# Differential attention: plain identity transposes, 1/sum moved into the next norm, and the product with V in plain float32

## The chip, the core and the metric

One core of a Trainium2 chip runs the whole program as one launch. The metric is the device time of one execution in microseconds. The three runs of the kernel before took 3952.47 us in the median (3940.81 to 3964.31).

## What is computed

Two blocks in a row. The first (a Hyena and a gated recurrent mixer, then 16 experts) is not touched. The second has two layers over 1024 latent tokens and 256 context tokens; four heads, each with two score maps, and a norm over the 128 values of each head behind them:

```python
def rms_norm(t, g):
    y = tf * lax.rsqrt(jnp.mean(tf * tf, axis=-1, keepdims=True) + EPS)
...
def diff_attend(q, k, v, lam):
    s = jnp.einsum('bhmqd,bhmkd->bhmqk', q, k).astype(jnp.float32) * (QK_DIM ** -0.5)
    p = jax.nn.softmax(s, axis=-1)
    p = p[:, :, 0] - lam * p[:, :, 1]
    return jnp.einsum('bhqk,bhkd->bhqd', p.astype(v.dtype), v)

def attn_post(o, subln_g, lam_init):
    o = rms_norm(o, subln_g) * (1.0 - lam_init)
```

The latent queries see 256 context keys and 1024 latent keys. In the first layer the context also attends to itself (256 queries, 256 keys).

## The kernel before

The program is written as tiles in pools with a fixed number of buffers; a scheduler lists the instructions of each engine in an order made at build time, and each engine then runs its list in order. `interleave` and generators set in which order the text hands out the work; a tile's buffer is handed on when its readers are done.

Nearly all products are made from halves: a float32 operand is split into a rounded part (F32R, by ScalarE in `split`, line 184) and the remainder (VectorE or GpSimd, line 187), and `mm3` (lines 204 to 206) adds three rounded matmuls. `mm` (line 209) is one matmul; with plain float32 operands it leaves two records in a trace, with F32R operands one. `tr` (line 212) is the transpose of a block by the identity. In names like `po<-th,Vh` the first operand moves, the second is the one held in the array.

`lat_path` runs the two latent layers. Each first projects v, q and k (`v_rows`, `qk_rows`) and makes the two side branches (`side_ct`), then come attention and the gate projection together, then the output projection with the norm (`gated_y`, `out_pair`). The context attention, `ctx_rest`, runs inside the expert layer, beside `moe`.

`lat_operands` loads K and V of one head. K is split into two stacked operands (KA), V into Vh and Vl, through `u2` tiles that hold the raw loads. All loads go over SP's queue in order (`self.dma`).

`attention` walks over blocks of 256 queries, 4 a head, 16 a layer. In each, for two groups of 128 queries and both maps: scores in pieces of 512, 512 and 256 keys (tile `s`, six matmuls), a VectorE copy with the scale and a running minimum (`E`, line 1515), the minimum over the pieces, the exponential on ScalarE with its sum (line 181), then 1/sum (line 1522) and the difference of the two maps: on VectorE for the second group, on ScalarE and GpSimd for the first. Then, for five pairs of key tiles, the weights are turned: four matmuls by a diagonal matrix `dg` that holds -1/sum, made on GpSimd from a negated identity (`nident`); so the turning also scales. The turned block `pt` is split into `th` (ScalarE) and `tl` (VectorE), and six matmuls add it times V into `po`:

```python
                        self.mm(pt[:, kk, i * 128:i * 128 + 128], Ps[i][:, (kp + kk) * 128:(kp + kk) * 128 + 128], dgs[i])
...
                self.cp(th, pt)
                self.tt(tl, pt, th.bitcast(F32), SUB)
...
                    self.mm3(po, V[0][:, kt], V[1][:, kt], th[:, kk], tl[:, kk], kt == 0, kt == nkt - 1)
```

Between these steps `next(fill, None)` hands out one step of the gate projection (`gate_steps`: three matmuls of 512 columns, tile `po<-T`); 24 of its 128 steps stand ahead of the attention (`FRONT`), 9 are called for in each block. `gated_y` takes the attention's output of 256 tokens, sums the squares per head and token, makes the root of the mean plus eps (`rstd`) and scales by it and by `sub`, which is subln_g times (1 - lam_init).

Of the kernel before, what the change touches and what calls it, by code (L numbers as in the profile page):

```python
# [9 lines left out]
F32 = mybir.dt.float32  # L10
F32R = mybir.dt.float32r
# [9 lines left out]
EPS = 1e-6  # L21
# [109 lines left out]
class Work:  # L131
# [1304 lines left out]
    def ctx_operands(self, h):  # L1436

        KA = [self.t("cKA", [128, 256], F32R) for _ in range(2)]
        QA = [self.t("cQA", [128, 256], F32R) for _ in range(2)]
        QB = [self.t("cQA", [128, 256], F32R) for _ in range(2)]  # L1440
        V = (self.t("cV", [128, 2, 128], F32R), self.t("cV", [128, 2, 128], F32R))
        k, q, v = (self.t("cu", [128, 256]) for _ in range(3))
# [4 lines left out]
        v = v.rearrange("p (a b) -> p a b", a=2)  # L1447
        self.dma(v, self.dvc[0, h])
        self.split(v, *V)
        return KA, lambda qb: (QA, QB), V, self.rqc[h]  # L1450

    def ctx_qk(self, l, q, h, hT, w="w"):
# [6 lines left out]

    def lat_operands(self, l, h):  # L1460
        KA = [self.t("KA", [128, 1280], F32R) for _ in range(2)]
        V = (self.t("Vh", [128, 10, 128], F32R), self.t("Vl", [128, 10, 128], F32R))
        kc = self.t("u2", [128, 256])
        self.dma(kc, self.dkc[l, h])
        self.put_qk(kc, KA, None, slice(0, 256))
        for t0 in range(0, 1024, 512):
            kt = self.t("u2")
            self.dma(kt, self.dqk[h, 1][:, t0:t0 + 512])
            self.put_qk(kt, KA, None, slice(256 + t0, 768 + t0))
        q = self.t("qf")  # L1470
        self.dma(q, self.dqk[h, 0])
        vc = self.t("u2", [128, 2, 128])
        self.dma(vc, self.dvc[l, h])
        self.split(vc, V[0][:, 0:2], V[1][:, 0:2], self.nc.gpsimd)
        for t0 in range(0, 8, 4):
            vt = self.t("u2", [128, 4, 128])
            self.dma(vt, self.dv[h][:, t0:t0 + 4])
            s = slice(2 + t0, 6 + t0)
            self.split(vt, V[0][:, s], V[1][:, s], self.nc.gpsimd)

        def queries(qb):
            QA = [self.t("QA", [128, 256], F32R) for _ in range(2)]
# [6 lines left out]
    def attention(self, l, n, nk, ops, dst, c, fill=()):  # L1489


        fill = iter(fill)
        nc = self.nc
        KA, queries, V, rq = ops
        nkt = nk // 128
        chunks = [(k0, min(k0 + 512, nk)) for k0 in range(0, nk, 512)]
        nc_ = len(chunks)
        for qb in range(n // 256):
            QA, QB = queries(qb)
            Ps, dgs = [], []  # L1500
            for i in range(2):
                qs = slice(i * 128, i * 128 + 128)
                es = []
                mx = self.sm([128, 2, nc_ + 1], "a3")
                ss = self.sm([128, 2], "a2")
                rc = self.sm([128, 2], "a2")
                for m in range(2):
                    r = rq[:, qb * 2 + i, m:m + 1]
                    mc = mx[:, m, nc_:nc_ + 1]
                    E = self.t(c + "E%d" % m, [128, nk])  # L1510
                    for j, (k0, k1) in enumerate(chunks):
                        o = self.ps(c + "s", [128, k1 - k0])
# [7 lines left out]
                    self.act(E, E, AF.Exp, scale=-1.0, bias=mc, accum_out=ss[:, m:m + 1])  # L1520
                    es.append(E)
                nc.vector.reciprocal(rc, ss)  # L1522
                self.stt(rc[:, 1:2], rc[:, 1:2], self.lams[l], ss[:, 0:1], MUL, MUL)
                dg = self.t(c + "dg", [128, 128])
                self.ts(dg, self.nident, rc[:, 0:1], MUL, eng=nc.gpsimd)
                if c or i:
                    self.stt(es[0], es[1], rc[:, 1:2], es[0], MUL, SUB)
                else:
                    self.act(es[1], es[1], AF.Copy, scale=rc[:, 1:2])
                    self.tt(es[0], es[1], es[0], SUB, nc.gpsimd)  # L1530
                Ps.append(es[0])
                dgs.append(dg)
# [158 lines left out]
            lo.append(l_)  # L1691
        return hi, lo

    def gated_y(self, l, t0, dy, dg, pt, tag, ytag, tmp):

        hi, lo = [], []
        tsl = slice(t0, t0 + 256)
        for cc in range(2):
# [5 lines left out]
            if cc:  # L1704
                pm = self.ps(pt, [128, 2, 4])
                for c2 in range(2):
                    sq = self.t(tmp, [128, 2, 256])
                    self.act(sq, y[:, c2 * 2:c2 * 2 + 2], AF.Square)
                    for i in range(2):
                        for hh in range(2):  # L1710
                            h = c2 * 2 + hh
                            self.mm(pm[:, i, h:h + 1], sq[:, hh, i * 128:i * 128 + 128], self.ones[:, 0:1])
                rs = self.sm([128, 2, 4], "gy")
# [67 lines left out]
            self.dma(self.f256, I["k_f256"])  # L1781

    def prep2(self, pt, tmp):
        self.nident = self.cst([128, 128], name="nident")
        self.ts(self.nident, self.ident, -1.0, MUL)
# [45 lines left out]
    def ctx_rest(self):  # L1831
# [1 line left out]
        dyc, dgc = self.dyc, self.dgc  # L1833
        P_ = self.nc.gpsimd
        with ExitStack() as e:
            self.open(e, "right", cKA=4, cQA=6, cV=4, cE0=2, cE1=2, cdg=2, cth=1, ctl=1, cot=1)
            for h in range(4):
                yield from self.attention(0, 256, 256, self.ctx_operands(h), dyc[4 + h], "c")
        with ExitStack() as e:
            self.open(e, "right", cy=4)  # L1840
            y = self.gated_y(0, 0, dyc, dgc, "cp", "cy", "Tc", "cv")
# [65 lines left out]
    def lat_path(self, hT, rope, ec, e0, e1):  # L1907
# [3 lines left out]
        for l in range(2):  # L1911
# [22 lines left out]
                        self.side_ct(l, 1024, hT, dy, SH.index(h), "sp", "su", "sw", "sz")  # L1934
            ec.close()
            Tl = "T%d" % l
            with ExitStack() as e2:
                self.open_ps(e2, "left", po=2, pt=2, s=4)
                self.open(e2, "left", KA=4, qf=2, QA=8, E0=4, E1=2, u2=3, wr=2, wh=2, wl=2, gu=2,
                          Vh=2, Vl=2, dg=4, th=2, tl=2, ot=2, gb=1)  # L1940
                gate = self.gate_steps(l, 1024, hT, dg, "po", "gu", "w", self.nc.gpsimd)
                for _ in range(FRONT):
                    next(gate)
                for h in range(4):
                    ops = self.lat_operands(l, h)
                    for _ in self.attention(l, 1024, 1280, ops, dy[4 + h], "", gate):
                        pass
                for _ in gate:
                    pass
# [4 lines left out]
            with ExitStack() as e2:  # L1954
                self.open_ps(e2, "left", pp=3, pq=5)
                self.open(e2, "left", y4=5, yt=6, xr=3, u2=4)
                dst = self.dram([1024, 1024], name="x3") if l == 0 else self.out[0]
                gy = lambda t0: self.gated_y(l, t0, dy, dg, "pq", "y4", "yt", "u2")
# [226 lines left out]
```

## Time and profile before

| | |
|---|---|
| runs (3) | 3952.47 us median, 3940.81 to 3964.31 |
| the profiled execution | 3952.19 us, its span 3950.4 us |
| TensorE busy (PE) | 3602.6 us, 91% |
| VectorE (DVE) / ScalarE (ACT) / GpSimd (POOL) busy | 2909.2 / 2305.5 / 1293.6 us |
| moved by DMA | 824.40 MB, mean 209 GB/s |
| latent attention, layer 0 | 2830 to 3165 us |
| latent attention, layer 1 | 3512 to 3844 us |

Busy time of TensorE counts overlapping matmuls once; a matmul's own duration includes its way through the array, so its price in a row of matmuls is the distance of their starts. "PEclk" is the granted TensorE clock, 1.00 for the full 2.4 GHz, 0.50 for 1.2 GHz; a value between is a mean over time. "Idle before" is time in which the engine waited, with what ended it.

### The profile page before, as it was taken

The page shows a single profiled execution, that of the slowest core. Times are in us where ns is not written, and L with a number is a line of the kernel's source. Part 1 is how long each engine was busy: PE and PEld are TensorE (multiplying, and loading weights), DVE is VectorE, ACT ScalarE, POOL GpSimd, SP SyncE. Part 2 cuts the span into 40 slices and gives each one's busy share as a digit, 9 for nine tenths or more (in the row PEclk, how much of TensorE's full clock was granted, in tenths as well). Part 3 has the DMA queues.
Part 4 walks back from the last instruction along what each step waited for, and adds up shares of the span by engine and source line. Part 5 has one row for each costly group of instructions (what it writes and reads, how often), then busy time and mean ns, then how long its engine had stood idle before and what let it go on. Part 6 is the DMA issues. An engine that isn't in the chain of part 4 may idle for free. (4 is left out here: it accounts for less than half of the span.)

```text
span 3950.4 us, 54906 instructions
## 1 busy us (share of the span) xinstructions
PE 3602.6 (91%) x18922; PEld 2940.1 (74%) x18922; DVE 2909.2 (74%) x4414; ACT 2305.5 (58%) x3757; POOL 1293.6 (33%) x940
## 2 busy tenths in 40 slices
PE   6999899768897899999999999879999899999989
PEld 2667688646866778787777777678788788878878
DVE  4587778898635898889888888855677744567772
ACT  4443433355534787778777777665566654566762
POOL 3455655454413313230121120101444620143461
PEclk7999999879998999999999999989999999999989
DMA  7777767645376699999999999951311244131033
GB/s 230 224 220 222 221 211 222 212 165 190 115 253 204 213 330 350 351 323 352 365 355 365 365 353 364 318 179 52 121 50 39 71 139 120 60 119 58 33 102 112
DMA packets 530527, 824.40 MB, mean 209 GB/s; under 512 B 38193, under 2 KB 241991, under 8 KB 530248
## 3 DMA queue, kind: packets, MB, share of 16 engines
q1 hardware_dynamic: 503176, 755.74, 56.0%
q0 software_dynamic: 26048, 64.09, 6.0%
q8 instruction: 149, 2.44, 0.3%
q10 hardware_dynamic: 1024, 1.06, 0.2%
q14 instruction: 130, 1.06, 0.1%
HBM read 712.65 MB, written 107.05 MB: 207 GB/s over the span
## 5 line engine op out<-in xcount | busy, mean ns | idle before, releaser
L187 DVE TENSOR_TENSOR el<-er,eh 128x1024 fp32r<-128x1024 f32 x763 | 953.5, 1299 | 99.0 <-ACT eh L184 97.1
L184 ACT ACTIVATE eh<-er 128x1024 fp32r<-128x1024 f32 x768 | 785.5, 1057 | 128.3 <-PE ea L206 86.0
L205 PE MATMUL ea<-el,xh 128*128 128x512 f32 x1024 | 416.2, 406 | 22.9 <-DVE el L187 20.6
L206 PE MATMUL ea<-eh,xh 128*128 128x512 f32 x1024 | 405.2, 396 | 0.0
L204 PE MATMUL ea<-eh,xh 128*128 128x512 f32 x1024 | 404.3, 398 | 0.2 <-ACT eh L184 0.2
L1284 POOL DMA_INDIRECT acc<-yo,idx x16 | 76.6, 4786 | 761.8 <-DVE yo L196 761.8
L1515 DVE TENSOR_SCALAR_CACHE_REDUCE E<-s,rq 128x512 f32<-128x512 f32 (+1 forms) x384 | 239.1, 657 | 51.4 <-PE s L209 37.1
L205 PEld LDWEIGHTS ea<-el,xh 128*128 128x128 f32 x1024 | 192.7, 188 | 91.3 <-DVE el L187 50.6
L181 ACT ACTIVATE E<-E,a 128x1280 f32<-128x1280 f32 x160 | 216.6, 1359 | 57.0 <-DVE a L1519 52.9
L209 PE MATMUL s<-KA,QA 128*128 128x512 f32 (+1 forms) x768 | 203.0, 387 | 26.7 <-DVE E L1515 26.0
L204 PEld LDWEIGHTS ea<-eh,xh 128*128 128x128 f32 x1024 | 192.7, 188 | 46.0 <-ACT eh L184 0.9
L206 PEld LDWEIGHTS ea<-eh,xh 128*128 128x128 f32 x1024 | 193.0, 188 | 38.7
L205 PE MATMUL ey<-el,hh 128*128 128x512 f32 x512 | 205.3, 401 | 3.4 <-DVE el L187 3.3
L204 PE MATMUL ey<-eh,hh 128*128 128x512 f32 x512 | 202.7, 403 | 4.2 <-ACT eh L184 4.0
L206 PE MATMUL ey<-eh,hh 128*128 128x512 f32 x512 | 202.2, 395 | 0.0
L209 PE MATMUL pt<-dg,E 128*128 128x128 f32 x1280 | 181.9, 288 | 10.6 <-DVE E L196 4.5
L184 ACT ACTIVATE u<-pp 32x512 f32<-32x512 f32 (+2 forms) x212 | 124.2, 587 | 99.3 <-PE pp L206 93.0
L204 PE MATMUL pp<-T,ah 128*128 128x512 f32 x448 | 180.4, 403 | 0.0
L209 PEld LDWEIGHTS pt<-dg,E 128*128 128x128 f32 x1280 | 168.6, 203 | 15.8 <-issue 11.9
L205 PE MATMUL pp<-T,ah 128*128 128x512 f32 x448 | 177.8, 397 | 0.0
L206 PE MATMUL pp<-T,al 128*128 128x512 f32 x448 | 177.3, 396 | 0.0
L187 POOL TENSOR_TENSOR wl<-wr,wh 128x1024 fp32r<-128x1024 f32 (+1 forms) x48 | 117.6, 2459 | 179.2 <-ACT wh L184 177.8
(535 smaller groups left out, 10003.8 us busy)
## 6 DMA issues: line engine op xcount, KB each, us to landing
er<-in_exp_w_dram SPq DMA_DIRECT2D x768, 512.0 KB
wr<-in_w_in_dram SPq DMA_DIRECT2D x60, 512.0 KB
dc<-in_k_dft_dram POOLq DMA_DIRECT2D x72, 384.0 KB, 4.4
dc<-in_k_dft_dram POOLq DMA_DIRECT2D x72, 256.0 KB, 4.4
ar<-in_w_in_dram SPq DMA_DIRECT2D x64, 256.0 KB
mr<-in_w_mod_dram SPq DMA_DIRECT2D x48, 256.0 KB
wr<-in_ada_w_dram SPq DMA_DIRECT2D x24, 512.0 KB
wr<-in_w_out_dram SPq DMA_DIRECT2D x24, 512.0 KB
```

The costliest lines, as they stand in the source:

```text
L181: return self.nc.scalar.activation(out, in_, func, **kw)
L184: return self.nc.scalar.activation(out, in_, AF.Copy)
L187: return (eng or self.nc.vector).tensor_tensor(out, a, b, op=op)
L204: mm(out, lh, rh, start=first, stop=False)
L205: mm(out, lh, rl, start=False, stop=False)
L206: mm(out, ll, rh, start=False, stop=last)
L209: self.nc.tensor.matmul(out, l, r, start=first, stop=last)
L1284: nc.gpsimd.indirect_dma_start(out=self.acc, out_offset=x[0], in_=yo, in_offset=None, compute_op=ADD)
L1515: nc.vector.tensor_scalar(E[:, k0:k1], o, r, None, op0=MUL, op1=ALU.min, accum_out=mx[:, m, j:j + 1] if nc_ > 1 else mc)
```

## The change

The transposes use the identity and carry no scale. The two maps are combined as (lambda x sum0/sum1) x E1 - E0, which is minus sum0 times the wanted weights; the sign goes into `sub` (lam_init - 1). The factor sum0 cancels in the norm behind, if its eps is multiplied by sum0 squared: so the sums are kept in a constant tile `s0` per layer, and `gated_y` uses eps x s0 x s0, by two more small VectorE operations and a square root without its bias. V is loaded once, unsplit; `th` stays plain float32; `tl`, `dg`, `Vh`, `Vl` and `nident` are gone; the product with V is one `mm` per key tile in place of `mm3`. `th` has 4 buffers instead of 2.

```diff
@@ ctx_operands and lat_operands: V
-        V = (self.t("Vh", [128, 10, 128], F32R), self.t("Vl", [128, 10, 128], F32R))
+        V = self.t("V", [128, 10, 128])
+        self.dma(V[:, 0:2], self.dvc[l, h])
+        self.dma(V[:, 2:10], self.dv[h])
...
-        vc = self.t("u2", [128, 2, 128])
-        self.dma(vc, self.dvc[l, h])
-        self.split(vc, V[0][:, 0:2], V[1][:, 0:2], self.nc.gpsimd)
-        for t0 in range(0, 8, 4):
-            vt = self.t("u2", [128, 4, 128])
-            self.dma(vt, self.dv[h][:, t0:t0 + 4])
-            s = slice(2 + t0, 6 + t0)
-            self.split(vt, V[0][:, s], V[1][:, s], self.nc.gpsimd)
@@ attention
-                ss = self.sm([128, 2], "a2")
-                rc = self.sm([128, 2], "a2")
+                sums = [s0[:, qb * 2 + i:qb * 2 + i + 1], self.sm([128, 1], "a2")]
+                rc = self.sm([128, 1], "a2")
...
-                nc.vector.reciprocal(rc, ss)
-                self.stt(rc[:, 1:2], rc[:, 1:2], self.lams[l], ss[:, 0:1], MUL, MUL)
-                dg = self.t(c + "dg", [128, 128])
-                self.ts(dg, self.nident, rc[:, 0:1], MUL, eng=nc.gpsimd)
+                nc.vector.reciprocal(rc, sums[1])
+                self.stt(rc, rc, self.lams[l], sums[0], MUL, MUL)
...
-                        self.mm(pt[:, kk, i * 128:i * 128 + 128], Ps[i][:, (kp + kk) * 128:(kp + kk) * 128 + 128], dgs[i])
-                th = self.t(c + "th", [128, 2, 256], F32R)
-                tl = self.t(c + "tl", [128, 2, 256], F32R)
+                        self.tr(pt[:, kk, i * 128:i * 128 + 128], Ps[i][:, (kp + kk) * 128:(kp + kk) * 128 + 128])
+                th = self.t(c + "th", [128, 2, 256])
                 self.cp(th, pt)
-                self.tt(tl, pt, th.bitcast(F32), SUB)
...
-                    self.mm3(po, V[0][:, kt], V[1][:, kt], th[:, kk], tl[:, kk], kt == 0, kt == nkt - 1)
+                    self.mm(po, V[:, kt], th[:, kk], kt == 0, kt == nkt - 1)
@@ gated_y
-                self.rstd(rs, pm, 128, "gy")
+                rs, sd = (self.sm([128, 2, 4], "gy") for _ in range(2))
+                i0 = t0 // 128
+                si = s0[:, :, i0:i0 + 2].rearrange("p h i -> p i h")
+                self.stt(sd, si, EPS, si, MUL, MUL)
+                self.stt(rs, pm, 1.0 / 128, sd, MUL, ADD)
+                self.act(sd, rs, AF.Sqrt)
+                self.nc.vector.reciprocal(rs, sd)
@@ prep2
-            self.ts(s, self.colb("subln_g_2", l), 1.0 - LAM_INIT[l], MUL)
+            self.ts(s, self.colb("subln_g_2", l), LAM_INIT[l] - 1.0, MUL)
@@ lat_path
-                          Vh=2, Vl=2, dg=4, th=2, tl=2, ot=2, gb=1)
+                          V=2, th=4, ot=2, gb=1)
```

The scheduler makes a new order. TensorE at the end of layer 0's attention (last block of the last head; `pt` the turned weights, `E` the weights, `po` the sum with V), first before:

```order
L209 MATMUL pt_29981<-dg_29878,E_7466_29846 128x128
L209 MATMUL pt_29981<-dg_29917,E_7478_29885 128x128
L204 MATMUL po_29920<-th_29971,Vh_29293 128x256
L205 MATMUL po_29920<-tl_29972,Vh_29293 128x256
L206 MATMUL po_29920<-th_29971,Vl_29294 128x256
L204 MATMUL po_29920<-th_29971,Vh_29293 128x256
L205 MATMUL po_29920<-tl_29972,Vh_29293 128x256
L206 MATMUL po_29920<-th_29971,Vl_29294 128x256
```

and the same place now:

```order
L212 MATMUL pt_29319<-ident_116,E_7321_29221 128x128
L212 MATMUL pt_29319<-ident_116,E_7332_29258 128x128
L209 MATMUL po_29291<-th_29315,V_28781 128x256 x2
L212 MATMUL pt_29328<-ident_116,E_7321_29221 128x128
L212 MATMUL pt_29328<-ident_116,E_7332_29258 128x128
```

Six matmuls behind two tiles, th and tl, have become two (x2) behind one, and the transposes of the next pair still stand between them.

SP's queue ahead of the attention of layer 0 (`qf` the queries, `u` from dkc and dqk the keys, `u` from dvc and dv the values, all of head 0, but the second qf of head 1), before:

```order
L177 DMA qf_26789<-dqk_24849 128x1024
L177 DMA qf_27634<-dqk_24849 128x1024
...
L177 DMA u_6700_26771<-dkc_10007 128x256
L177 DMA u_6701_26777<-dqk_24849 128x512
...
L177 DMA u_6704_26791<-dvc_10009 128x256
L177 DMA u_6705_26795<-dv_24850 128x512
```

and now:

```order
L177 DMA V_26698<-dvc_10009 128x256
L177 DMA V_26698<-dv_24787 128x1024
...
L177 DMA V_27396<-dvc_10009 128x256
L177 DMA V_27396<-dv_24787 128x1024
...
L177 DMA qf_26719<-dqk_24786 128x1024
L177 DMA qf_27417<-dqk_24786 128x1024
```

The loads of V of heads 0 and 1 have moved from behind the key loads to ahead of the query loads.

## Rows read from the trace of the kernel before

**Rows 1.** The page, first line.
```profile
span 3950.4 us, 54906 instructions
```

**Rows 2.** Busy time by stretch: us, engines (instructions), PEclk, DMA share, GB/s.
```profile
2830.00:3165.00 335.00, 302.77 (x1821) 263.26 (x1820) 250.24 (x659) 221.70 (x357) 165.27 (x110) 0.95 0.20 65
3512.00:3844.00 332.00, 301.11 (x1820) 263.21 (x1819) 253.43 (x657) 224.15 (x360) 169.80 (x112) 0.94 0.21 66
...
2830.00:2870.00 40.00, 30.64 (x124) 23.62 (x123) 28.82 (x82) 27.04 (x43) 21.86 (x17) 0.83 0.41 129
2870.00:3080.00 210.00, 201.97 (x1252) 176.88 (x1250) 158.09 (x418) 138.80 (x229) 89.69 (x64) 0.99 0.15 49
3080.00:3165.00 85.00, 70.17 (x450) 62.77 (x449) 63.33 (x161) 55.87 (x86) 53.72 (x30) 0.90 0.23 73
```

**Rows 3.** PE's waits in layer 0: us in total, times, longest.
```profile
PE s L209 <- DVE E L1515: 13.4, 10, 2.8
PE po L205 <- DVE tl L187: 8.1, 8, 4.2
PE po L204 <- ACT th L184: 4.0, 5, 1.9
```

**Rows 4.** PE's waits in layer 1.
```profile
PE po L205 <- DVE tl L187: 10.8, 8, 4.2
```

**Rows 5.** Timeline of PE, layer 0: start, length, line, out<-in, shape, count.
```profile
2899.84 0.28 PE L204 MATMUL po<-th,Vh 128*128 128x256 f32 x1
2899.96 0.28 PE L205 MATMUL po<-tl,Vh 128*128 128x256 f32 x1
...
2906.73 1.73 PE L209 MATMUL pt<-dg,E 128*128 128x128 f32 x14
2908.21 0.48 PE L205 MATMUL po<-T,wh 128*128 128x512 f32 x1
2908.52 0.39 PE L206 MATMUL po<-T,wl 128*128 128x512 f32 x1
2908.75 0.63 PE L209 MATMUL s<-KA,QA 128*128 128x512 f32 x2
```

**Rows 6.** PE's groups by shape in layer 0: records, busy us, mean ns, idle before.
```profile
L209 PE MATMUL pt<-dg,E 128*128 128x128 f32 x640 | 90.9, 287 | 5.3 <-DVE E L196 2.2 <-DVE a L1522 2.0 <-POOL E L187 0.8
L209 PE MATMUL s<-KA,QA 128*128 128x512 f32 x256 | 85.1, 431 | 9.5 <-DVE E L1515 8.9 <-DVE KA L187 0.4
L205 PE MATMUL po<-tl,Vh 128*128 128x256 f32 x160 | 48.9, 306 | 8.3 <-DVE tl L187 8.1
...
L204 PE MATMUL po<-T,wh 128*128 128x512 f32 x105 | 42.1, 401 | 0.5 <-ACT ot L184 0.5
```

**Rows 7.** Timeline of PE, transposes in the output stage of layer 0.
```profile
3203.21 1.25 PE L212 MATMUL pq<-ident,y 128*128 128x128 f32 x10
3204.22 0.48 PE L205 MATMUL pp<-T,yt 128*128 128x512 f32 x1
3204.54 0.40 PE L206 MATMUL pp<-T,yt 128*128 128x512 f32 x1
```

**Rows 8.** Timeline of PE, plain float32 with 256 columns, first stage.
```profile
134.83 10.63 PE L209 MATMUL pp<-c,cr 128*128 128x256 f32 x48
```

**Rows 9.** VectorE's group tl in layer 0.
```profile
L187 DVE TENSOR_TENSOR tl<-pt,th 128x512 fp32r<-128x512 f32 x80 | 54.6, 686 | 29.3 <-ACT th L184 29.2
```

**Rows 10.** Timeline of PE, tail of layer 0.
```profile
3099.36 0.58 PE L205 MATMUL po<-tl,Vh 128*128 128x256 f32 x1 [4.22 <-DVE tl L187]
```

**Rows 11.** ScalarE's group Vh in layer 0.
```profile
L184 ACT ACTIVATE Vh<-u 128x512 fp32r<-128x512 f32 x8 | 5.0, 620 | 7.2 <-DMA u<-dv 7.2
```

**Rows 12.** Timeline of ScalarE, a table load at layer 0's end.
```profile
3158.09 1.28 ACT L181 ACT_TABLE_LOAD   x1
```

**Rows 13.** Busy time by stretch, in the expert layer.
```profile
2350.00:2450.00 100.00, 96.92 (x427) 75.81 (x426) 90.12 (x83) 76.08 (x92) 19.08 (x5) 1.00 1.01 355
```

**Rows 14.** Timeline of PE, transposes behind a long idle time.
```profile
2582.86 3.92 PE L212 MATMUL fp<-ident,xn 128*128 128x128 f32 x16 [25.29 <-DVE xn L192]
```

More of the change, by code (lines that the diff above doesn't have):

```diff
@@ L1440, in ctx_operands @@
         QB = [self.t("cQA", [128, 256], F32R) for _ in range(2)]
-        V = (self.t("cV", [128, 2, 128], F32R), self.t("cV", [128, 2, 128], F32R))
-        k, q, v = (self.t("cu", [128, 256]) for _ in range(3))
+        V = self.t("cV", [128, 2, 128])
+        k, q = (self.t("cu", [128, 256]) for _ in range(2))
         self.dma(k, self.dkc[0, h])
@@ L1446, in ctx_operands @@
         self.put_qk(q, QA, QB, slice(0, 256))
-        v = v.rearrange("p (a b) -> p a b", a=2)
-        self.dma(v, self.dvc[0, h])
-        self.split(v, *V)
+        self.dma(V, self.dvc[0, h])
         return KA, lambda qb: (QA, QB), V, self.rqc[h]
@@ L1487, in lat_operands, with attention @@
         return KA, queries, V, self.rq[h]
-    def attention(self, l, n, nk, ops, dst, c, fill=()):
+    def attention(self, l, n, nk, ops, dst, s0, c, fill=()):
         fill = iter(fill)
@@ L1499, in attention @@
             QA, QB = queries(qb)
-            Ps, dgs = [], []
+            Ps = []
             for i in range(2):
@@ L1519, in attention @@
                         nc.vector.tensor_reduce(mc, mx[:, m, :nc_], axis=AX.X, op=ALU.min)
-                    self.act(E, E, AF.Exp, scale=-1.0, bias=mc, accum_out=ss[:, m:m + 1])
+                    self.act(E, E, AF.Exp, scale=-1.0, bias=mc, accum_out=sums[m])
                     es.append(E)
-                nc.vector.reciprocal(rc, ss)
-                self.stt(rc[:, 1:2], rc[:, 1:2], self.lams[l], ss[:, 0:1], MUL, MUL)
-                dg = self.t(c + "dg", [128, 128])
-                self.ts(dg, self.nident, rc[:, 0:1], MUL, eng=nc.gpsimd)
+                nc.vector.reciprocal(rc, sums[1])
+                self.stt(rc, rc, self.lams[l], sums[0], MUL, MUL)
                 if c or i:
-                    self.stt(es[0], es[1], rc[:, 1:2], es[0], MUL, SUB)
+                    self.stt(es[0], es[1], rc, es[0], MUL, SUB)
                 else:
-                    self.act(es[1], es[1], AF.Copy, scale=rc[:, 1:2])
+                    self.act(es[1], es[1], AF.Copy, scale=rc)
                     self.tt(es[0], es[1], es[0], SUB, nc.gpsimd)
                 Ps.append(es[0])
-                dgs.append(dg)
             po = self.ps(c + "po", [128, 256])
@@ L1692, in w_gated, with gated_y @@
         return hi, lo
-    def gated_y(self, l, t0, dy, dg, pt, tag, ytag, tmp):
+    def gated_y(self, l, t0, dy, dg, s0, pt, tag, ytag, tmp):
         hi, lo = [], []
@@ L1712, in gated_y @@
                             self.mm(pm[:, i, h:h + 1], sq[:, hh, i * 128:i * 128 + 128], self.ones[:, 0:1])
-                rs = self.sm([128, 2, 4], "gy")
-                self.rstd(rs, pm, 128, "gy")
+                rs, sd = (self.sm([128, 2, 4], "gy") for _ in range(2))
[5 more added lines that the diff above has]
+                self.nc.vector.reciprocal(rs, sd)
                 for c2 in range(2):
@@ L1783, in prep2 @@
     def prep2(self, pt, tmp):
-        self.nident = self.cst([128, 128], name="nident")
-        self.ts(self.nident, self.ident, -1.0, MUL)
         self.lams = [self.lam(l, tmp) for l in range(2)]
@@ L1835, in ctx_rest @@
         with ExitStack() as e:
-            self.open(e, "right", cKA=4, cQA=6, cV=4, cE0=2, cE1=2, cdg=2, cth=1, ctl=1, cot=1)
+            self.open(e, "right", cKA=4, cQA=6, cV=2, cE0=2, cE1=2, cth=2, cot=1)
+            s0 = self.cst([128, 4, 2], name="s0")
             for h in range(4):
-                yield from self.attention(0, 256, 256, self.ctx_operands(h), dyc[4 + h], "c")
+                yield from self.attention(0, 256, 256, self.ctx_operands(h), dyc[4 + h], s0[:, h], "c")
         with ExitStack() as e:
             self.open(e, "right", cy=4)
-            y = self.gated_y(0, 0, dyc, dgc, "cp", "cy", "Tc", "cv")
+            y = self.gated_y(0, 0, dyc, dgc, s0, "cp", "cy", "Tc", "cv")
             gb = self.t("cy")
@@ L1936, in lat_path @@
             Tl = "T%d" % l
+            s0 = self.cst([128, 4, 8], name="s0")
             with ExitStack() as e2:
@@ L1945, in lat_path @@
                     ops = self.lat_operands(l, h)
-                    for _ in self.attention(l, 1024, 1280, ops, dy[4 + h], "", gate):
+                    for _ in self.attention(l, 1024, 1280, ops, dy[4 + h], s0[:, h], "", gate):
                         pass
@@ L1957, in lat_path @@
                 dst = self.dram([1024, 1024], name="x3") if l == 0 else self.out[0]
-                gy = lambda t0: self.gated_y(l, t0, dy, dg, "pq", "y4", "yt", "u2")
+                gy = lambda t0: self.gated_y(l, t0, dy, dg, s0, "pq", "y4", "yt", "u2")
                 y = gy(0)
```

## Prediction

> **What bounds the kernel now.** The profiled execution took 3952.19 us, 1.79 us more than its span [rows 1], and stands 0.3 us under the median of the three runs, so the sum below is made from it. The edits act in three places: the context attention (inside the expert layer), the two latent attention layers, and the small norm behind each. I read first the stretches of the two layers [rows 2]. From the first scores to the last product with V the layers take 335 and 332 us. Within layer 0 three stretches differ: a start of 40 us with mean granted clock 0.83, a middle of 210 us in which the steps of the gate projection fill every gap (TensorE busy 202 of 210, clock 0.99), and a tail of 85 us after the gate has run out (TensorE 70, VectorE 63, clock 0.90). No other engine reaches TensorE's share: in the whole layer 0 VectorE is busy 250 us, ScalarE 222, GpSimd 165.
>
> Next, TensorE's waits [rows 3, 4]: in layer 0 it waits 13.4 us for score copies (E), 8.1 for tl, 4.0 for th; in layer 1 10.8 for tl. Small against 335, so the layer is bound by what TensorE has to do, most of all in the middle.
>
> What it has to do is read from starts, since a matmul's length overlaps its neighbour's. Rounded operands (the halves) of 256 columns start 0.12 us apart, of 512 columns 0.23; the 14 records of plain float32 transposing matmuls take (2908.52 - 2906.73 - 0.23)/14 = 0.111 each [rows 5]. The counts per layer [rows 6]: 640 records write pt, which is 320 matmuls of two records each; 160 each of three kinds write po (480); 256 scores of 512 columns; 3 x 105 gate steps; by the code 128 scores of 256 columns. That is 71.3 + 57.6 + 58.9 + 72.5 + 15.4 = 275.7 us at the full level of 2.4 GHz in 335 us. The remaining 59 us are waits, the start and stretches at the lower level.
>
> **The change, part by part.**
>
> *Transposes.* 320 matmuls by the diagonal dg become 320 transposes by the identity. The trace has the same operation in a later stage: ten in 3204.54 - 3203.21 - 0.23 = 1.10 us, 0.110 each, one record [rows 7]. 71.3 becomes 35.2: -36.1 us a layer.
>
> *Product with V.* 480 matmuls of rounded halves (57.6 us) become 160 plain ones, two records each. The nearest row with this shape, plain float32 with 256 columns, is the stretch of 48 records in 10.63 us, 0.22 each [rows 8]: 320 x 0.22 = 70.4, so +12.8 us a layer. Its bounds: 0.111 a record (the price at 128 columns [rows 5], 36 us in all) and 0.24 (two steps of a rounded matmul of this width, 77 us); rows 8 have the very shape, so I take them. Net -23.3 us a layer, **-47 us** in both. I count it in full: in the middle nothing else is near its limit, and in the tail VectorE, second there, loses even more. The Trainium skill (FP8 and Floating Point Precision, the note on true FP32) says that such a matmul takes four passes through the array where the halves took three. By that rule the product alone costs 57.6 x 4/3 = 76.8, an estimate, and the two layers would gain 34 us in place of 47; the rows, at 0.44 against 0.36 us, show a factor of 1.2.
>
> *tl goes.* 80 VectorE subtractions of 0.686 us a layer [rows 9], 110 us in all, from an engine with slack; what counts is that the matmuls no longer wait for them: 8.1 + 10.8 = 18.9 us of TensorE. In the tail one such wait was 4.22 us, and the matmul behind it took 0.58 us [rows 10], where 0.28 is usual [rows 5]: the clock had fallen. Next in line is th, the ScalarE copy, which still has to come; half of the wait should pass to it. I take -10, bounds 0 and -19.
>
> *Clock.* Both start and tail sit at 0.83 to 0.90 [rows 2]. With shorter waits some of this returns: -4 us, bounds 0 and -10.
>
> *V.* The halves of V are no longer made: 12 ScalarE copies and 12 GpSimd subtractions a layer, and GpSimd has no dg to make either. ScalarE, in order, waited 7.2 us at the start of layer 0 for V's data [rows 11], with score work behind. The V loads now go straight to their tile, 8 pairs of two in place of 8 groups of three, the same bytes; SP issues those of heads 0 and 1 ahead of the q loads. They wait for a buffer freed by the previous stage; the head's q and k loads stand behind them. -3 us, bounds -10 and +5 (the queue held once per layer).
>
> *Norm.* Behind each layer two tiny VectorE operations are added per block of 256 tokens and the order has four more table loads on ScalarE, 1.28 us each [rows 12]. The block is prepared one ahead of its use, under matmuls; I take +1, bounds 0 and +6.
>
> *Context.* The same edits, 16 transposes and 8 products, lie in the expert layer, where the DMA engines are busy 1.01 of the time and VectorE 0.90 [rows 13]. The transfers hide it: 0, bounds -5 and +2.
>
> Sum: -47 - 10 - 4 - 3 + 1 = -63, so **3889 us**.
>
> **Rivals.**
>
> *A new wait takes most of it.* With less for TensorE to do, the chain scores, minimum, exponential, subtraction, transposes, th has less cover, and ScalarE (222 us a layer, its exponentials and th copies unchanged) becomes what the matmuls wait for. For it: TensorE already waits for th and E [rows 3]. Against: ScalarE would be at 0.7 of a shortened layer, and VectorE answers sooner. Price: half of the 47 us and none of the rest: 3952 - 24 = 3928.
>
> *More comes back.* All of 18.9 us on tl, 10 us of clock and 10 at the starts: 3952 - 47 - 19 - 10 - 10 - 3 = about 3863. For it: the tail's TensorE is only 83% busy and the longest waits there are for tl [rows 3, 10].
>
> *The clock falls: slower.* Sixteen transposes, after 25.29 us of idle, ran 3.92 us, 0.245 each, over twice the price of rows 7 [rows 14], so at the 1.2 GHz level; if a pass of the identity did less to lift or hold the clock than the plain matmuls it replaces, the middle would lose its 0.99. Price: with start and tail wholly at the lower level, their share of the new work, 252 - 183 = 69 us a layer (183 is the middle's 200 x 252.4/275.7), takes 138 in place of 125; with a mean of 0.85 in the middle that takes 192/0.85 = 226 in place of 210. That is +29 a layer, 4010 us. It decides where, with start and tail fallen, the middle's clock comes under about 0.97 (192/0.97 = 198, 12 less than now, and 13 more outside). Against: the ten transposes of rows 7 run at full pace between matmuls, and here groups of four last 0.44 us, a seventh of TensorE's work. The Trainium skill (TensorE: Matmul & The Clock Gate, Part 4: PE-mode transpose) speaks for this rival: the fast clock does not engage for transposes, which do not count as work in the way a matmul does. The rows bear it out only after a long idle time.
>
> *It does not show.* The order of the engines is made by a scheduler; were its new order to add as many in-order stalls as it saves (the V loads that hold SP's queue, transposes ahead of a late th), the time stays near 3950.
>
> **How the numbers follow.** Forecast (3870 to 3905) 0.64; half of it (3928) 0.15; more (3863) 0.12; no effect 0.05; clock 0.04. A measurement of this kernel tells about 0.5%, 20 us, from no change. Faster by over that needs less than 3932: the forecast, the larger gain and most of the half, 0.64 + 0.12 + 0.13 = 0.89; within it the rest of the half and no effect, 0.07; slower 0.04. The range from 3860 to 3928 takes the forecast, the half and the larger gain, 0.85 or more with their own spread, and leaves out the last two cases.
>
> **What would show it.** Right: 320 records of pt a layer at 0.11 us and 320 of po at 0.22; the layers' stretches about 30 us shorter each, the middle still over 0.95 busy at a clock near 0.99; no wait on tl, a longer one on th. Wrong: po records over 0.24 us; a middle with clock under 0.97; TensorE's waits on th or E in a layer above 30 us together (they are 17.4 in layer 0); the stages outside the two layers moved by over 10 us.

## The result, and the profile of the changed kernel

The changed kernel takes 3904.13 us (median of four runs, 3901.16 to 3905.45), the kernel before beside it 3946.64 us: a ratio of 0.9892, 95% interval 0.987 to 0.9914. That is 42.5 us faster where 63 were forecast, inside the range (3860 to 3928) and of the sign forecast. The profiled execution took 3905.45 us, 46.7 less than the one of before (3952.19), from which the forecast's sum was made.

The page of the changed kernel, span and busy time of the engines (answers to rows 1):

```profile
span 3903.6 us, 52551 instructions
...
PE 3554.2 (91%) x17938; PEld 2859.8 (73%) x17938; DVE 2829.5 (72%) x4263; ACT 2290.4 (59%) x3733; POOL 1206.4 (31%) x844
```

VectorE fell by 80 us and GpSimd by 87, TensorE by 48, close to the 47 of the forecast's work. The span fell by about as much (46.8), but as a balance of gains and losses in several stages, shown below. Busy time by stretch (as rows 2; layer 0 whole, its first 40 us, the part up to the gate's end, the tail; then layer 1):

```profile
2833.00:3140.00 307.00, 276.32 (x1341) 221.38 (x1340) 213.78 (x575) 212.43 (x344) 128.90 (x67) 0.96 0.19 61
2833.00:2873.00 40.00, 35.94 (x162) 28.13 (x161) 30.02 (x89) 27.51 (x43) 13.75 (x8) 0.91 0.26 87
2873.00:3057.00 184.00, 175.11 (x872) 143.42 (x871) 123.30 (x341) 127.75 (x212) 63.79 (x36) 0.98 0.15 50
3057.00:3140.00 83.00, 65.27 (x310) 49.83 (x309) 60.45 (x148) 57.17 (x90) 51.36 (x24) 0.93 0.23 75
3491.00:3796.00 305.00, 276.21 (x1345) 221.46 (x1343) 215.33 (x578) 215.38 (x348) 133.93 (x68) 0.95 0.21 67
```

The layers are 28 us shorter each. The start does 36 us of work in 40 where it did 31. The tail is somewhat looser than it was: 18 of its 83 us are idle, where it was 15 of 85.

TensorE's waits in layer 0, then in layer 1 (as rows 3 and 4):

```profile
PE s L209 <- DVE E L1507: 15.5, 15, 3.0
PE po L209 <- ACT th L184: 8.3, 9, 2.2
PE pt L212 <- DVE E L196: 6.5, 6, 1.8
```
```profile
PE s L209 <- DVE E L1507: 17.0, 16, 3.0
PE po L209 <- ACT th L184: 7.0, 7, 2.3
PE pt L212 <- DVE E L196: 4.7, 5, 1.3
```

There is no tl, but these lines, which are all of either view, sum to 30.3 and 28.7 us; all lines of the same views of before sum to 31.7 and 30.5. Of before, the lines of layer 0 behind those of rows 3, then layer 1's other large ones:

```profile
PE pt L209 <- DVE E L196: 2.2, 3, 1.3
PE pt L209 <- DVE a L1522: 2.0, 1, 2.0
```
```profile
PE s L209 <- DVE E L1515: 12.5, 11, 2.8
PE pt L209 <- DVE E L196: 2.3, 3, 1.3
PE po L204 <- ACT th L184: 1.4, 2, 1.1
```

What went at tl came back at the score copies (s, for E), at th and at the difference of the maps (pt, for E).

The price of one instruction, from starts (timeline of TensorE, layer 0):

```profile
2890.09 0.87 PE L212 MATMUL pt<-ident,E 128*128 128x128 f32 x6 [1.75 <-DVE E L196]
2890.76 1.14 PE L209 MATMUL s<-KA,QA 128*128 128x256 f32 x4
2891.74 1.03 PE L209 MATMUL po<-th,V 128*128 128x256 f32 x4
2892.60 0.60 PE L212 MATMUL pt<-ident,E 128*128 128x128 f32 x4
2892.96 0.48 PE L204 MATMUL po<-T,wh 128*128 128x512 f32 x1
```

Six transposes in 0.67 us are 0.112 each (the four behind the product, 0.36 us to the next start, even less); four records of the product in 0.86 are 0.215, or 0.43 for one product. The Trainium skill (FP8 and Floating Point Precision, TensorE Precision Notes) gives true FP32 four passes through the array; against the three rounded matmuls of the halves, 0.36 us, that is an estimate of 0.48. The trace has 0.43.

The whole program cut at six events that every run has, by first and last starts like these (changed kernel; the last product of the router, the first transposes behind the experts, then first scores and last product with V of layer 0):

```profile
L209 PE MATMUL pq<-rw,m x128: 177/263/397, 1124.2 to 1233.4; 128*128 128x16 f32 x128
...
L212 PE MATMUL fp<-ident,xn x64: 270/273/477, 2584.3 to 2635.0; 128*128 128x128 f32 x64
...
L209 PE MATMUL s<-KA,QA x384: 274/395/796, 2833.3 to 3123.6; 128*128 128x512 f32 x128, 128*128 128x256 f32 x64
...
L209 PE MATMUL po<-th,V x320: 377/379/634, 2858.8 to 3139.3; 128*128 128x256 f32 x160
```

So the expert layer is 2584.3 - 1233.4 = 1350.9 us and layer 0 is 306.0. The same rows of the kernel before:

```profile
L209 PE MATMUL pq<-rw,m x128: 177/263/397, 1130.4 to 1239.2; 128*128 128x16 f32 x128
...
L212 PE MATMUL fp<-ident,xn x64: 272/273/476, 2582.9 to 2633.9; 128*128 128x128 f32 x64
```

1343.7 us there. All kernels of this study in this cut (us of the profiled execution; the last column is the difference of the medians, against the kernel before on the same chip). The stages are those of one execution each, and not always of a typical one: with 7 gate steps it is the fastest of five, 12 us under the median, with the context in halves and 8 steps the slowest of five, 9 above it, with the halves kept the slowest, 7 above.

| kernel | experts | to scores | layer 0 | between | layer 1 | end | median less before |
|---|---|---|---|---|---|---|---|
| before | 1343.7 | 247.4 | 334.3 | 348.0 | 331.4 | 106.4 | |
| changed | 1350.9 | 249.0 | 306.0 | 352.3 | 303.7 | 108.3 | -42.5 |
| changed again | 1351.0 | 249.8 | 304.0 | 350.7 | 304.5 | 106.5 | -43.3 |
| halves kept | 1342.4 | 247.5 | 313.9 | 355.5 | 310.4 | 107.2 | -46.0 |
| diagonal kept | 1349.4 | 250.3 | 332.9 | 354.9 | 340.0 | 106.4 | +14.1 |
| plain eps | 1351.6 | 249.0 | 304.8 | 352.5 | 305.7 | 106.4 | -46.4 |
| 7 gate steps | 1348.2 | 249.1 | 291.9 | 362.5 | 293.1 | 110.9 | -52.0 |
| 8 gate steps | 1351.2 | 249.0 | 297.2 | 349.8 | 297.1 | 106.5 | -56.4 |
| difference on VectorE | 1348.5 | 249.2 | 299.3 | 355.8 | 301.9 | 111.2 | -47.6 |
| context in halves | 1341.8 | 247.5 | 311.7 | 344.6 | 311.9 | 107.4 | -48.7 |
| halves, 8 steps | 1343.6 | 246.2 | 325.6 | 346.7 | 329.6 | 106.4 | -12.0 |
| context in halves, 8 steps | 1342.6 | 248.6 | 305.4 | 352.0 | 296.6 | 106.8 | -68.9 |
| the same, difference on VectorE | 1339.9 | 246.4 | 301.8 | 350.5 | 302.2 | 107.6 | -65.6 |
| context buffers | 1348.9 | 249.3 | 303.7 | 350.7 | 302.8 | 106.5 | -50.4 |

The stretch up to the router, which no edit touches, differs by up to 11 us from run to run (1231 to 1242) and is left out. So the profiled gain of 46.8 of span is 56.0 in the two layers, 5.8 of that chance at the front, and 15.0 given back: 8.8 up to the first scores, 4.3 between the layers, 1.9 at the end.

One thing moves across these marks. In four kernels (diagonal kept, 7 gate steps, context in halves, halves with 8 steps) the first scores of layer 1 come before the last 8 of the 24 gate steps that otherwise stand ahead of them (112 of the 128 in the layer, where the others have 104 or 105): 24 matmuls of 0.23 us, so some 5.5 us of their column "layer 1" belong to "between".

### The profile page after: what moved, and what is told of

Same layout as the page of the kernel before. It is cut to its first block, busy times and chain, and to the rows that moved or that the text cites. A ratio compares the mean times of both kernels' runs of the same rounds, so it can differ in the third digit from the quotient of the medians.

```text
span 3903.6 us, 52551 instructions
## 1 busy us (share of the span) xinstructions
PE 3554.2 (91%) x17938; PEld 2859.8 (73%) x17938; DVE 2829.5 (72%) x4263; ACT 2290.4 (59%) x3733; POOL 1206.4 (31%) x844
## 3 DMA queue, kind: packets, MB, share of 16 engines
q1 hardware_dynamic: 502024, 755.74, 56.4%
## 5 line engine op out<-in xcount | busy, mean ns | idle before, releaser
L209 PE MATMUL s<-KA,QA 128*128 128x512 f32 (+1 forms) x768 | 213.0, 401 | 33.0 <-DVE E L1507 32.5
L209 PEld LDWEIGHTS s<-KA,QA 128*128 128x128 f32 x768 | 134.3, 202 | 76.0 <-DVE E L1507 57.8
L209 PE MATMUL po<-th,V 128*128 128x256 f32 x640 | 168.7, 389 | 15.3 <-ACT th L184 15.3
```

The costliest lines, as they stand in the source:

```text
L209: self.nc.tensor.matmul(out, l, r, start=first, stop=last)
```

## The experiments

**The transposes alone.** The product with V goes back to th, tl, Vh and Vl, V's loads and splits too, and th to 2 buffers.

```diff
+                self.tt(tl, pt, th.bitcast(F32), SUB)
...
-                    self.mm(po, V[:, kt], th[:, kk], kt == 0, kt == nkt - 1)
+                    self.mm3(po, V[0][:, kt], V[1][:, kt], th[:, kk], tl[:, kk], kt == 0, kt == nkt - 1)
```

> The transposes by the identity and 1/sum in the norm alone; the product with V is again made of rounded halves (th, tl, Vh, Vl). Theory A (the gain is TensorE's work, counted in full, and the waits taken away came back as others): a layer loses 36.1 us of TensorE's work and gains none, so about 72 us less in the layers and some 9 given back outside them, a time 60 to 72 us below the kernel before and 15 to 25 us below the changed kernel. Rival B (a good part of the gain is the work that VectorE, ScalarE and GpSimd no longer do for the halves): no faster than the changed kernel, 25 to 45 us below the kernel before.

Measured: 3906.76 us, ratio 0.9877 (0.986 to 0.9893), no faster than the changed kernel, 46 us below the kernel before. That is what rival B said (25 to 45 below, with the noise), and theory A's number failed: 36.1 us of work less gave 20.4 and 21.0 us a layer. Its layer 0 in the three stretches (start, up to the gate's end, tail), and its waits:

```profile
2824.00:2864.00 40.00, 30.24 (x114) 22.75 (x113) 31.02 (x81) 27.04 (x43) 18.32 (x14) 0.79 0.39 124
2864.00:3053.00 189.00, 178.62 (x1028) 151.59 (x1027) 152.14 (x410) 133.95 (x224) 75.22 (x44) 0.97 0.15 50
3053.00:3139.00 86.00, 65.17 (x361) 54.82 (x359) 69.23 (x167) 59.40 (x91) 54.66 (x24) 0.87 0.27 85
```
```profile
PE s L209 <- DVE E L1515: 15.6, 12, 3.7
PE po L205 <- DVE tl L187: 14.7, 11, 5.8
PE pt L212 <- DVE E L196: 4.4, 4, 2.2
PE po L204 <- ACT th L184: 4.4, 6, 1.9
```

With less for TensorE to do, the waits for tl rise from 8.1 to 14.7 us (from 10.8 to 15.8 in layer 1), and the clock's means are 0.79, 0.97 and 0.87 where rows 2 of the kernel before have 0.83, 0.99 and 0.90. VectorE is busy 69 of 86 us in the tail.

**The plain product alone.** The diagonal, its scale and the old norm stay (the line below is against the changed kernel).

```diff
-                        self.tr(pt[:, kk, i * 128:i * 128 + 128], Ps[i][:, (kp + kk) * 128:(kp + kk) * 128 + 128])
+                        self.mm(pt[:, kk, i * 128:i * 128 + 128], Ps[i][:, (kp + kk) * 128:(kp + kk) * 128 + 128], dgs[i])
```

> The other half alone: the product with V in plain float32 with V loaded once, but the transposes still by the diagonal with -1/sum and the norm as before. Theory A: 12.8 us more of TensorE's work a layer, less some 5 us a layer in the start where V is no longer split: slower than the kernel before by 10 to 26 us. Rival B: faster than the kernel before by 10 to 30 us.

Measured: 3966.85 us, ratio 1.0028 (1.0016 to 1.004): slower by 14, as theory A said, but not where it said it. The layers grew by 7.2 us together under 25.6 us more work, and 5.5 of the 7.2 are the gate steps of layer 1 named above; so the product gives back some 12 us a layer and costs about nothing there. Most of the loss lies elsewhere: between the layers, with those steps counted there, the profiled execution takes 12.4 us more than the kernel before (TensorE idle 12.0 us where it was 6.8, mean clock 0.97 where it was 0.99), and in the expert layer 5.7. One place where the product gives back is the start:

```profile
2835.00:2875.00 40.00, 35.65 (x169) 28.24 (x168) 28.50 (x85) 26.03 (x40) 15.27 (x12) 0.91 0.24 76
```

35.65 us of work at a clock of 0.91, as in the changed kernel, though the diagonals are there; with the halves kept it is 30.24 at 0.79. So what fills the start comes with the plain product and not with the transposes. Of its parts, V loaded whole and not split is the likely one; it was not tried alone.

The two runs together: neither theory fits both. Alone, the transposes gave 41 us in the layers; with the plain product in place (from this run to the changed kernel) they gave 26.9 in layer 0 and, less the gate steps, 30.8 in layer 1. The two edits act on each other.

**The norm.** `gated_y` uses the plain eps again and so leaves out the factor sum0 squared.

```diff
-                self.stt(sd, si, EPS, si, MUL, MUL)
-                self.stt(rs, pm, 1.0 / 128, sd, MUL, ADD)
-                self.act(sd, rs, AF.Sqrt)
-                self.nc.vector.reciprocal(rs, sd)
+                self.rstd(rs, pm, 128, "gy")
```

> The changed kernel with the norm's eps left plain (the factor sum0 squared is left out, two small VectorE operations and a table load fewer per block of 256 tokens). If the 4 us by which the stage between the layers and the 2 us by which the end grew are the norm's, 4 to 7 us below the changed kernel; if they are the clock's at the exit of the layer (mean 0.76 in the first 25 us behind layer 0), within 2 us of it.

Measured: 3906.38 us, ratio 0.9877 (0.9861 to 0.9894); between the layers 352.5 us, as in the changed kernel (352.3 and 350.7). The norm costs nothing that shows there; the medians alone could not tell the 4 us. What lengthens that stage in part is a lower clock behind the layer (25 us from its end on, first the kernel before, then the changed one):

```profile
3165.00:3190.00 25.00, 24.33 (x138) 20.70 (x137) 8.23 (x12) 12.33 (x18) 8.03 (x3) 1.00 0.40 138
```
```profile
3140.00:3165.00 25.00, 24.84 (x107) 21.09 (x108) 6.60 (x12) 12.51 (x16) 4.78 (x3) 0.76 0.39 133
```

Both are full of work, but the second runs at a mean of 0.76, 6 us lost. In the changed kernel's second profile it was 0.86 (3.5 us).

**The gate's steps, 7 a block.** The filler lasts longer.

```diff
-                next(fill, None)
+                if kp < 6:
+                    next(fill, None)
```

> The changed kernel with 7 steps of the gate called for in each block in place of 9, so that they last to the end of the layer. Theory A with a tail that is bound by the chain of one block (TensorE busy 65 of 83 us, 17.7 idle): the steps fill the tail's gaps and hold the clock there, the middle loses a little of its cover: 10 to 25 us below the changed kernel. If the tail is bound by VectorE and ScalarE (60 and 57 of 83 us) and the gaps only move to the middle: within 5 us of it.

Measured: 3900.72 us, ratio 0.9863 (0.9843 to 0.9883), its runs from 3888.55 to 3906.49: inconclusive as a time. The profile, of its fastest run, tells more: the layers are 14.1 and (less the gate steps named above) 16.1 us shorter than the changed kernel's, and 15.7 are given back between them, most of it in one wait:

```profile
3118.45 2.17 PE L209 MATMUL po<-th,V 128*128 128x256 f32 x8
3135.02 1.23 PE L209 MATMUL pq<-ones,u 128*128 128x1 f32 x5 [14.39 <-ACT u L181]
```

The scheduler had put the first loads of y behind the attention's last store on SP's queue; in the changed kernel they stand ahead of it.

**The changed kernel again, and three variants on its chip.** First the same text:

> The changed kernel once more, word for word, beside the three that follow, so that they can be compared with it on one chip: 40 to 50 us below the kernel before. For the expert layer: if the 7 us by which it grew come with the change and not from one execution to the next, the distance from the last product of the router (pq<-rw) to the first transposes behind the experts (fp) is again over 1349 us (1351 in the changed kernel, 1344 before).

3907.11 us, ratio 0.9883 (0.9863 to 0.9904), and the expert layer takes 1351.0 us again.

Next, only the context attention's product in halves (the latent layers plain):

```diff
-                    self.mm(po, V[:, kt], th[:, kk], kt == 0, kt == nkt - 1)
+                    if c:
+                        self.mm3(po, V[0][:, kt], V[1][:, kt], th[:, kk], tl[:, kk], kt == 0, kt == nkt - 1)
+                    else:
+                        self.mm(po, V[:, kt], th[:, kk], kt == 0, kt == nkt - 1)
```

> The changed kernel with only the context attention's product with V as before (halves, V split, eight products of six matmuls); the two latent layers unchanged. If the plain product in the context is what lengthened the expert layer (1344 us to 1351), 5 to 9 us below the changed kernel, all of it in the expert layer; if it is a matter of the order that the scheduler made, or of the execution, within 3 us of it.

3901.65 us, ratio 0.9871 (0.9853 to 0.9889), 5.5 us below the run beside it, with intervals that overlap. The trace is plain:

```profile
L209 PE MATMUL pq<-rw,m x128: 177/263/393, 1127.9 to 1238.7; 128*128 128x16 f32 x128
...
L212 PE MATMUL fp<-ident,xn x64: 270/273/476, 2580.5 to 2631.5; 128*128 128x128 f32 x64
```

1341.8 us. Down the table, the six kernels with halves in the context have 1339.9 to 1343.7 us (the kernel before among them), the eight with the plain product 1348.2 to 1351.6, without overlap. Some of the 9 us is lost again in layer 0 and what follows (1075.6 us from first scores to the end, where the changed kernel has 1070.3 and 1065.7).

The loads of the expert weights (768 issues of `er` on SP's queue, in time from the router's last product) show where in the stage the loss arises. The 11th is issued at the same time in both kernels, to 0.1 us; the 101st at 239.1 us in the changed kernel against 234.2 with the context in halves; the 301st at 605.2 against 593.8; the last at 1308.2 against 1298.4. So the loads fall behind in the first 600 us, beside the context attention (its products with V run from 124 to 233 us) and the context's work that follows it; from there on both keep the same pace, 703 and 705 us for the rest.

Then the difference of the two maps on VectorE for both groups:

```diff
-                if c or i:
-                    self.stt(es[0], es[1], rc, es[0], MUL, SUB)
-                else:
-                    self.act(es[1], es[1], AF.Copy, scale=rc)
-                    self.tt(es[0], es[1], es[0], SUB, nc.gpsimd)
+                self.stt(es[0], es[1], rc, es[0], MUL, SUB)
```

> The changed kernel with the difference of the two maps on VectorE for both groups of 128 queries (before, the first one on ScalarE and GpSimd): 16 copies of 1.36 us leave ScalarE and 16 subtractions of 3.03 us GpSimd in each layer, 16 of some 1.6 us come to VectorE, which is busy 214 of 306 us. If TensorE's waits are the chain of one block (scores, minimum, exponential, difference, transposes, th), the chain is some 3 us shorter in each block and the layers 5 to 10 us shorter each; if they are VectorE's share (the waits for score copies, 15 and 17 us a layer), the layers grow by 3 to 8 us each.

3902.81 us, ratio 0.9878 (0.9861 to 0.9895): no difference that can be told. The layers are 4.7 and 2.6 us shorter than in the run beside it, the stages behind them 5.1 and 4.7 longer.

Last, 8 gate steps a block:

```diff
-                next(fill, None)
+                if kp:
+                    next(fill, None)
```

> The changed kernel with 8 steps of the gate called for in each block (9 in it, 7 in the run before), and SP's queue with the loads of the norm's first operands (y) ahead of the attention's last store, as in the changed kernel; with 7 they stood behind it in layer 0 and TensorE waited 14.4 us there. Theory (the tail's gaps are filled by the gate's steps, and the loss with 7 was that order): the layers 5 to 12 us shorter each, nothing given back behind layer 0, 10 to 20 us below the changed kernel. If steps moved into the tail only take from the middle what they give: within 4 us of it.

3893.99 us, ratio 0.9852 (0.983 to 0.9873), 13 us below the changed kernel beside it (their intervals just overlap: 0.9863 to 0.9904 there), with layers 6.8 and 7.4 us shorter and nothing given back behind layer 0. Its stretches (start, up to the gate's end, tail):

```profile
2842.00:2882.00 40.00, 35.92 (x163) 28.18 (x162) 30.37 (x90) 27.87 (x44) 13.68 (x8) 0.91 0.27 89
2882.00:3066.00 184.00, 180.43 (x932) 149.52 (x931) 131.25 (x379) 138.67 (x231) 67.12 (x38) 1.00 0.15 50
3066.00:3139.00 73.00, 53.52 (x244) 42.45 (x243) 46.46 (x108) 46.87 (x72) 48.03 (x22) 0.86 0.26 86
```

The middle takes the same 184 us and does 180 us of work in it in place of 175, at a clock of 1.00; the uncovered tail is 10 us shorter and no denser than it was.

**Combinations.** The halves with 8 steps (both edits above):

> The run with the halves kept (transposes by the identity, the product of rounded halves everywhere) and 8 gate steps a block in place of 9. If its waits for tl (14.7 and 15.8 us a layer, 12.2 of the first in the tail) are there for want of cover, the steps that now last longer halve them and this run gains more than the plain product did from the same edit (13 us): 15 to 25 us below the halves with 9 steps. If the chain through tl is the bound itself, it gains no more than 10 us and stays above the plain product with 8 steps.

3937.18 us, ratio 0.9973 (0.9963 to 0.9984): a loss stood in neither branch. It is 30 us slower than the halves with 9 steps, 34 when each is taken against the kernel before beside it. Its waits in layer 0:

```profile
PE s L209 <- DVE E L1515: 24.8, 14, 4.3
PE po L205 <- DVE tl L187: 16.7, 10, 5.3
PE po L204 <- ACT th L184: 5.0, 6, 1.5
```

Two edits that each save time elsewhere lose together: the layers took 325.6 and 329.6 us. In layer 0 TensorE is idle for 52.8 us, where it is 40.8 with 9 steps. Why the order that comes of it is so much worse was not taken apart.

The plain product in the latent layers, the context in halves, 8 steps:

> Both gains together: the plain product in the latent layers with 8 gate steps a block, and the context's product of halves as before. If the two are independent: 5 us below the plain product with 8 steps (ratio to the kernel before about 0.984), with 1342 us from router to the transposes behind the experts and layers near 297 us. If the scheduler's new order takes it back as it did in part with 9 steps (layer 1 and the end were 7 us longer there): the same as with 8 steps alone.

3880.27 us, ratio 0.9823 (0.981 to 0.9836): the fastest, 69 us below the kernel before, and its interval lies clear of the changed kernel's second one (0.9863 to 0.9904). Against 8 steps alone it is 12 us better by the medians (their intervals just overlap). The expert layer has its 1342.6 us; layer 0 is 8 us longer than with 8 steps alone, but that is read from the slowest of the five executions.

With the difference on VectorE as well:

> The run before with the difference of the two maps on VectorE for both groups as well. With 9 steps that edit made the layers 6.7 and 1.8 us shorter and the stages behind them longer by as much; the same expected here: within 5 us of the run before it, layers 292 to 297 us.

3883.6 us, ratio 0.9832 (0.9819 to 0.9845): the same time, as expected, though the layers took 301.8 and 302.2 us and not 292 to 297.

Last, the changed kernel with the context's buffers as before:

```diff
-            self.open(e, "right", cKA=4, cQA=6, cV=2, cE0=2, cE1=2, cth=2, cot=1)
+            self.open(e, "right", cKA=4, cQA=6, cV=4, cE0=2, cE1=2, cth=1, cot=1)
```

> The changed kernel with four buffers for V in the context attention in place of two, and one for the turned weights in place of two, as the kernel before had them. If the 7 us in the expert layer come from loads of V that wait for a buffer at the head of SP's queue, with the expert weights behind them: router to transposes 1342 to 1345 us, 5 to 8 us below the changed kernel. If not (the plain product itself, or the order the scheduler makes with it): 1349 to 1352 us again, within 3 us of it.

3898.81 us, ratio 0.988 (0.9862 to 0.9897); experts 1348.9 us. A lack of buffers for V is not what costs the 7 us. Which wait in the expert layer it is stays open: the product's work cannot be it, 8 products at 0.07 us more. Open too is how much of any difference here is the edit's own: every edit makes the scheduler list the instructions anew, and no run holds the order fixed.

## Why the prediction was right, and where it was not

The sign and the range held. The sum (-63) was 20 us too good by the medians, 16 by the profiled executions: 8 of these in the layers (-56 for -64), 8 outside them (15.0 given back, less the 5.8 of chance, where the sum had +1).

TensorE's time in a layer can be split into its work (busy time, with time at the lower level counted half), what the lower level cost while it was busy, and its idle time, from the clock and the instructions of each trace (us, layer 0 and layer 1):

| kernel | work | lost to the clock | idle |
|---|---|---|---|
| before | 287.4, 285.7 | 14.6, 14.8 | 32.2, 30.9 |
| changed | 263.9, 262.5 | 11.4, 12.5 | 30.7, 28.8 |
| halves kept | 251.5, 250.4 | 21.5, 20.4 | 40.8, 39.6 |
| diagonal kept, gate steps of layer 1 taken off | 297.5, 294.5 | 11.8, 15.5 | 23.6, 24.5 |

*Net work, -23.3 us a layer "in full".* It came: 23.5 and 23.2. This is the step on which the forecast rests, and it held for the whole change. That nothing was lost of it is luck in part, since neither half of it counts in full by itself.

*Transposes, -36.1 us a layer.* The price held: 0.112 us, one record, and the work alone fell by 35.9 and 35.3. That it counts in full did not: alone, it gave 20.4 and 21.0 us. "In the middle nothing else is near its limit" was read from shares of busy time. Take 36 us away and 9 come back as waits, most for tl, and 6 to 7 as lower clock. That the gate's filler and the wide TensorE work had been the cover for these waits is the likely reading; the halves with 8 steps, which lose, show that it is not the whole of it. The rival "a new wait takes most of it" described this, with the wrong waiter: it was the wait on tl that grew, and only in the run with the halves.

*Product, +12.8 us a layer.* Its price held too: 0.215 us a record, and the work grew by 12.4 and 12.1. Added to the transposes it did not cost 12.8 us, it gained 7.9 and 6.7: the halves' copies, subtractions and loads that go with it are worth some 20 us a layer, about 10 as waits and 8 to 10 as clock, where the sum had 8.5 a layer (tl, clock and V, 17 in all). The 4 buffers of th, for 2, came with it and were not tried apart. So the two terms, -72 and +26, were -41 and -15 in the layers; taken in the other order, the product with all that goes with it first, they were -58 and about +2 (the sum had -72 and +9). Either way the transposes gave less than the sum had and the rest more, together -56 against the -64 of all terms there.

*tl, -10.* Against the kernel before, the sum of TensorE's waits fell by 1.4 and 1.8 us only, for E (15.5 and 17.0) and th are next in line; against the kernel that the transposes alone would have made, the waits fell by some 10 us a layer. The term was sized on a wait that the other edit was about to change.

*Clock, -4:* in the layers 3.2 and 2.3 us less are lost (the start rose from 0.83 to 0.91, the tail from 0.90 to 0.93); the stage behind layer 0 lost 3.5 to 6 us to the lower level. About nothing in all. *V, -3:* the first 40 us hold 5.3 us more work in layer 0 (35.9 against 30.6) and 2.8 more in layer 1 (34.3 against 31.5). As the idle time of the whole layers fell by 3.6 us only, most of this went again behind the start; the term was not measured by itself. *Norm, +1:* nothing that shows.

*Context, 0 (bounds -5 and +2).* This is the step that failed outright: 7 us in the expert layer. "The transfers hide it" did not hold. A stage bound by its loads was delayed all the same, since the loads themselves fell behind while the context's work ran; what held them up is not shown.

The rival on the clock did not occur: the transposes run at full pace, 0.112 us at a granted clock of 1.00, and the middle's mean is 0.98. The Trainium skill (TensorE: Matmul & The Clock Gate, Part 4: PE-mode transpose) says that the fast clock does not engage for transposes. The trace does not agree for transposes between matmuls: with a seventh of TensorE's work in that form the middle's mean was 0.97 with the halves kept, 0.98 in the changed kernel and 1.00 with 8 steps. My own sign of being wrong, waits on th or E above 30 us in a layer, was reached in layer 0 only if the waits for the differences count (30.3; without them 23.8), and the gain still came. Another sign, stages outside the layers that move by over 10 us, is reached only by those behind the router together (15.0); none moved by more than 7.2.

## What to carry to other kernels

Price two edits of one loop together and apart: here the transposes gave 21 us a layer alone and 29 with the plain product in place, and the product cost nothing or gained 7, by whether the transposes stood already, since the first made the waits that the second removed. An engine with over 95% busy time is not bound by its work alone: a saving there is worth what the other engines can answer. Where filler lies matters as well: 8 steps a block in place of 9 gave 13 us with the plain product and cost 30 with the halves. And read the order of the queues after each small change: 7 steps gave a wait of 14.4 us behind layer 0 and 8 steps none, by where the scheduler put the loads of y.

## What the runs showed of the hardware that was not expected

TensorE's clock can stay at the lower level for several us of unbroken work: the 25 us behind layer 0's tail, full of work, had a mean granted clock of 0.76 in one profile of the changed kernel and 0.86 in another, between the levels of 1.2 and 2.4 GHz, which is 3.5 to 6 us; in the kernel before it was 1.00 there. In the first of them TensorE came out of a wait of 2.20 us and its matmuls of 512 columns started 0.43 us apart up to 3148.3 us, then 0.23, and 0.43 once more from 3158.8 to 3162.2. What decides is not shown: with 8 steps the tail is no denser (53.5 of 73 us), and the clock behind it was 1.00. A plain float32 product of 256 columns costs 0.43 us against 0.36 for three rounded ones, so the fewer instructions (320 records for 480) cost more of TensorE's time.
